# Conditioning columns as fp32 products over two load queues, and mixer products on half of the k tiles ahead of the last column

## The chip, the cores and the metric

The kernel runs on one core of a Trainium2 chip. The metric is device time in microseconds, from three runs, of which the median is taken; beside it stands one profiled execution, whose trace is what the rows below come from.

## What is computed

Two layers of a hybrid block on 256 latent tokens and 256 context tokens, 1024 features, fp32 throughout. Each layer turns a conditioning vector (one for latents, one for context) into shift, scale and gate, normalizes, mixes the tokens with four branches, and runs a convolutional feed-forward:

```python
mod = silu(c) @ p['w_ada'] + p['b_ada']            # 6 x 1024 columns: sh1, sc1, g1, sh2, sc2, g2
h = rmsnorm(x, p['norm1_g']) * (1 + sc1) + sh1     # c for the latents, c_ctx for the context
u = split_in(h @ p['w_in'])                        # SSD, GQA, differential attention, RG-LRU
y = merge_branches(h, (ssd, gqa, diff, rglru * gelu(gate)), p)
x = x + g1 * y
x = x + g2 * conv_ffn(modulate(rmsnorm(x, p['norm2_g']), sh2, sc2), p)
```

What matters here is the first stage: the mixer's input h of layer 0 needs x, its statistics, and the shift and scale of layer 0, and these need 1 MB x 8 of the weight w_ada.

## The kernel before

**Number format.** Products of the mixer take three passes: `whl` splits a weight into a high part (a cast to fp32r on ACT, L256, or on VectorE, L258) and a low part (a subtraction, L251, on VectorE or POOL); `split` does the same for activations; `mm3` (L265) multiplies low by high, high by low and high by high, and adds in PSUM. `turn` (L317) says which split takes POOL and which takes VectorE's cast. There are four buffers for split weights (`ws`) and two for raw ones (`wp`, tile `w`).

**First stage** (L1189 to L1243). Shift and scale of layer 0's first norm are 2048 columns, packed into four columns c of 512, each of four chunks of 512 KB, 16 chunks `ada0` to `ada15`. Column 0 is the shift of the features of k tiles 0 to 3, column 1 their scale, columns 2 and 3 the same for k tiles 4 to 7. A chunk holds two k tiles of the product, so it is two products of the conditioning (2 wide, the stationary operand) with 512 columns. Columns 0 and 1 are plain fp32 products (L1226), columns 2 and 3 are split and take three passes (L1224). All chunks load on SyncE's queue; eleven have a buffer `wa` each, the other five share the four `bo` buffers, so `ada15` waits for `ada11`. x comes in four loads on ACT's queue (`load_x`, L276), the parameter tables pp and rp there too (`load_params`, L358). `place` (L1202) copies a column's two rows from PSUM, turns them with four transposes and writes them into `mods`.

**Norm.** `norm_stats` (L497) squares x on ACT, sums on VectorE, and `rstd` (L477) gives 1/rms by a product with ones (L484), a power on POOL (L489) and a product that spreads it (L493). `norm_coeffs` (L455) makes scale and shift from `mods`, for half of the k tiles at a time. `norm` (L511) goes over the halves of the tokens (context first) and in each over the 8 k tiles: x times 1/rms (L517, into one of three `fo` buffers), scale and shift (L519 on ACT or L521 on VectorE), a cast (L256) and a subtraction (L251, POOL or VectorE): 16 tiles of 128x256 in all.

**Mixer.** `rg_in` (L987) is first: `rgx0` and `rgx1`, 1 MB each, two outputs each, and each output is `fm` (L525) over 8 k tiles, with `halves=True` for one half of the tokens after the other (256 columns a product, 192 products in all), then a convolution (`conv`, L542: ACT at L544, VectorE at L552). `rg_pair` (L1008) takes rgx0's two channels (tile `bcm`; rgx1's is `xs`): gate products (L1021, L1024), ACT, VectorE, one square root on ACT (L1033), scans (L1041 to L1044). `kvdt` and `xbc` follow.

**Order.** The program is written in order, but a planner orders each engine's instructions by its own estimate of when they are ready, the written order deciding among ready ones; on the chip each engine then runs its list in order. `tc.issue_after(i)` puts what it covers behind instruction i on that engine. A DMA is issued by an engine's own instruction list, and waits there if it has to.

Of the kernel before, what the change touches and what calls it, by code (L numbers as in the profile page):

```python
# [207 lines left out]
def _build(ctx, nc, tc, I, out, dbg):  # L208
# [56 lines left out]
    def mm3(ps, a, b, start, stop):  # L265

        PE.matmul(ps, a.l, b.h, start=start, stop=False)  # L267
        PE.matmul(ps, a.h, b.l, start=False, stop=False)  # L268
        PE.matmul(ps, a.h, b.h, start=False, stop=stop)  # L269

# [36 lines left out]
    def wraw(l, name, pl=None, tag=None, bufs=None, queue=None):  # L307
        off, kt, cols = CH[name]
        w = pl.tile([128, kt * cols], F32, name=tag, bufs=bufs) if pl else wp.tile([128, 2048], F32, name="w")
        t = I[f"w{l}"]  # L310
        (nc.scalar if pl and queue is None else nc.sync).dma_start(
            w[:, :kt * cols], bass.AP(tensor=t.tensor, offset=t.offset + off, ap=[[kt * cols, 128], [1, kt * cols]]))
        return w[:, :kt * cols].rearrange("p (k c) -> p k c", k=kt)
# [140 lines left out]

    def norm_coeffs(p, mod, base, gname, nm, halves=1):  # L455

        a = par.tile([128, 8, 2], F32, name=f"A{nm}")
        sh = par.tile([128, 8, 2], F32, name=f"sh{nm}")
        b = p["bada"]
        for i in range(halves):  # L460
            k = slice(i * 8 // halves, (i + 1) * 8 // halves)
# [5 lines left out]
        return a, sh  # L467

# [41 lines left out]

    def norm(x, rs, a, sh):  # L511
        h = Mat(*(hp.tile([128, KT, T], F32R, name=f"h{i}") for i in "hl"))
        for v, r in rs.items():
            ts = slice(v * 256, v * 256 + 256)
            for k in range(KT):
                t = tt("fo", 256)
# [7 lines left out]

    def fm(ps, w, h, n, start=True, stop=True, halves=False):  # L525

        if halves and n > 256:
            for v in reversed(range(n // 256)):
                ts = slice(v * 256, v * 256 + 256)
                fm(ps[:, ts], w, h[:, :, ts], 256)  # L530
            return
        kn = w.h.shape[1]
        for k in range(kn):
            mm3(ps, w[:, k], h[:, k, :n], start and k == 0, stop and k == kn - 1)

# [19 lines left out]
    class Mixer:  # L555
# [430 lines left out]

        def rg_in(self, i, tag, bufs):  # L987

            l, p, h = self.l, self.p, self.h
            w = wcols(l, f"rgx{i}")  # L990
            xr = self.long([128, 2, T], tag, bufs)
            bws = []
            for c in range(2):
                cp = 2 * i + c
                ps = big()
                fm(ps, w[c], h, T, halves=True)
                conv(xr[:, c], ps, p["rcw"], p["rcb"], T, 4, cp, 4)
# [196 lines left out]
    cth = ap_.tile([128, KT, 2], F32, name="cth")  # L1194
    csp = ap_.tile([128, 2, KT, 2], F32R, name="csp")
    cm = Mat(csp[:, 0], csp[:, 1])
# [3 lines left out]
    split(cm, ccol, V)  # L1200
    x = load_x()
    def place(c, ps):  # L1202
# [7 lines left out]
        V.tensor_copy(mods[0][:, i0:i0 + 4], tp.rearrange("p (i v) -> p i v", v=2))  # L1210

    before = None
    for c in range(4):

        ps = small()
        for k in range(0, KT, 2):
            z = c * 4 + k // 2
            w = wraw(0, f"ada{z}", ap_ if z < 11 else bop, "wa" if z < 11 else "bo", 11 if z < 11 else 4, nc.sync)
            w = w.rearrange("p a (k c) -> p (a k) c", k=2)
            if c >= 2:  # L1220
                w = whl(w)
            for i in range(2):
                if c >= 2:
                    mm3(ps[0:2], cm[:, k + i], w[:, i], k + i == 0, k + i == KT - 1)  # L1224
                else:
                    PE.matmul(ps[0:2], ccol[:, k + i], w[:, i], start=k + i == 0, stop=k + i == KT - 1)  # L1226
            if k == 2 and before:
                place(*before)
        before = c, ps
        if c == 2:  # L1230
            p = load_params(0)
            r = norm_stats(x, T)
    place(*before)
    closed(q0)
    for l in range(DEPTH):
        full = l < DEPTH - 1
        if l:
            p = load_params(l)
            with tc.high_priority():
                r = norm_stats(x, T)  # L1240
        with tc.issue_after(after[0, 4]) if l else nullcontext():
            a1, sh1 = norm_coeffs(p, mods[l], 0, "norm1", 1, 2)
        h = norm(x, r, a1, sh1)  # L1243
        early_params(l, p)
# [6 lines left out]
        b3 = mx.branch()  # L1251
        rin = [mx.rg_in(0, "bcm", 1), mx.rg_in(1, "xs", 2)]
        turn[1:] = 1, 2
# [68 lines left out]
        dbg(f"x{l}", x)  # L1322
        a2, sh2 = norm_coeffs(p, mods[l], 24, "norm2", 2)
        with tc.high_priority():
            h = norm(x, norm_stats(x, n), a2, sh2)
        fill = None
# [22 lines left out]
```

## Time and profile before

| what | us |
|---|---|
| median of three runs (1835.39 to 1839.09) | 1835.72 |
| the profiled execution | 1833.32 |
| its span, first to last instruction | 1831.2 |
| TensorE busy in the span | 1715.3 |
| VectorE, ACT, POOL busy | 1298.7, 904.4, 889.1 |

The profile gives each instruction's engine, line, tiles and times. A row of the timeline has its start and length in us, counted from the span's start; for several instructions merged into one row (xN) the length goes from the first start to the last end, or is their sum of covered time. Behind it, in brackets, stands the engine's idle time before the row and what ended it. "PE" is TensorE, "DVE" VectorE, "POOL" GpSimd, "SP" SyncE; a "q" behind an engine's name marks the issue of a DMA. A matmul's recorded length is longer than the step to the next one, as they are pipelined.

### The profile page before, as it was taken

To read this page: it belongs to the slowest core of one execution; us is meant where nothing else is said; L and a number is where in the kernel's file an instruction comes from. 1 tells how busy PE (TensorE), PEld (TensorE's weight loads), DVE (VectorE), ACT (ScalarE), POOL (GpSimd) and SP (SyncE) were. 2 spreads that over 40 slices of the span, in tenths; PEclk is the share of its full clock that TensorE was granted. 3 is DMA by queue.
4 is the path that set the end of the run, shared out by engine and by line. 5 is a ranking of instruction groups with operands and counts; after the bars stand their busy time and mean duration, and the time that the engine had idled before them with its cause. 6 is when DMAs were issued, how large, how long until landed. Compare 5 with 4: busy or idle time off the path is not lost.

```text
span 1831.2 us, 27922 instructions
## 1 busy us (share of the span) xinstructions
PE 1715.3 (94%) x10734; PEld 1499.3 (82%) x10734; DVE 1298.7 (71%) x2259; ACT 904.4 (49%) x1651; POOL 889.1 (49%) x536
## 2 busy tenths in 40 slices
PE   7968999999989998999999999966989999989999
PEld 1856788878788787987888888855888899989998
DVE  6798667666868676898856475698867668567664
ACT  3525544545444554465544343535445455556554
POOL 4364656252435657566543242465574244534443
PEclk8988999999989999999999999978989999989999
DMA  7211433131313355535645443222233133445553
GB/s 290 85 69 46 145 104 122 70 104 47 104 58 111 112 184 207 185 119 172 219 172 181 147 147 111 69 83 97 93 117 137 47 116 113 164 141 196 181 182 130
DMA packets 52036, 237.10 MB, mean 129 GB/s; under 512 B 9664, under 2 KB 12608, under 8 KB 34496
## 3 DMA queue, kind: packets, MB, share of 16 engines
q1 hardware_dynamic: 28080, 179.46, 28.1%
q10 hardware_dynamic: 23824, 55.86, 9.6%
q8 instruction: 85, 1.39, 0.3%
q14 instruction: 47, 0.39, 0.1%
HBM read 234.18 MB, written 1.11 MB: 128 GB/s over the span
## 4 chain that ended last, share of the span: by engine, by line
PE 44%; DVE 9%; DMA 2%; POOL 2%; ACT 2%; issue 2%; DVEq 0%; ACTq 0%; POOLq 0%; SPq 0%
PE big L267 13%; PE big L268 13%; PE big L269 13%; DVE whl L251 1%; DMA w<-in_w 1%; DVE fo L435 1%; POOL whl L251 1%; DVE fo L552 1%; DMA wa<-in_w 1%; PE small L781 1%; PE small L589 1%; ACT whl L256 1%; DVE whl L258 0%; DVE B L1044 0%; PE small L1021 0%
## 5 line engine op out<-in xcount | busy, mean ns | idle before, releaser
L251 POOL TENSOR_TENSOR whl<-w,whl 128x1024 fp32r<-128x1024 f32 (+3 forms) x194 | 453.8, 2342 | 525.8 <-ACT whl L256 428.5
L267 PE MATMUL big<-hh,whl 128*128 128x256 f32 (+1 forms) x1632 | 549.9, 341 | 25.6 <-POOL whl L251 22.7
L268 PE MATMUL big<-hl,whl 128*128 128x256 f32 (+1 forms) x1632 | 550.9, 339 | 0.8 <-POOL hl L251 0.8
L269 PE MATMUL big<-hh,whl 128*128 128x256 f32 (+1 forms) x1632 | 550.9, 339 | 0.0
L256 ACT CAST whl<-w 128x1024 fp32r<-128x1024 f32 (+2 forms) x314 | 308.5, 987 | 169.1 <-PE big L269 83.4
L267 PEld LDWEIGHTS big<-hh,whl 128*128 128x128 f32 x1632 | 313.2, 194 | 60.3 <-POOL whl L251 23.8
L268 PEld LDWEIGHTS big<-hl,whl 128*128 128x128 f32 x1632 | 314.3, 193 | 33.7 <-issue 2.8
L269 PEld LDWEIGHTS big<-hh,whl 128*128 128x128 f32 x1632 | 314.2, 193 | 33.1 <-issue 3.6
L251 DVE TENSOR_TENSOR whl<-w,whl 128x1024 fp32r<-128x1024 f32 (+2 forms) x150 | 206.3, 1377 | 68.6 <-ACT whl L256 68.3
L552 DVE SCALAR_TENSOR_TENSOR fo<-big,pp,fo 128x510 f32<-128x510 f32 (+2 forms) x224 | 141.4, 634 | 72.1 <-ACT fo L544 68.5
L431 POOL TENSOR_TENSOR wa<-wa,crow 128x1024 f32<-128x1024 f32 x48 | 125.9, 2626 | 75.5 <-DVE fo L435 44.2
L268 PE MATMUL big<-whl,hh 128*128 128x256 f32 (+1 forms) x512 | 149.6, 293 | 1.9 <-POOL whl L251 1.9
L267 PE MATMUL big<-whl,hl 128*128 128x256 f32 (+1 forms) x512 | 148.3, 291 | 2.3 <-DVE sq L1052 1.4
L269 PE MATMUL big<-whl,hh 128*128 128x256 f32 (+1 forms) x512 | 149.6, 293 | 0.0
L269 PE MATMUL big<-act,whl 128*128 128x256 f32 (+1 forms) x392 | 125.6, 321 | 0.0
L268 PE MATMUL big<-act,whl 128*128 128x256 f32 (+1 forms) x392 | 125.4, 320 | 0.0
L267 PE MATMUL big<-act,whl 128*128 128x256 f32 (+1 forms) x392 | 125.3, 320 | 0.0
L544 ACT ACTIVATE fo<-big,pp 128x512 f32<-128x512 f32 (+1 forms) x104 | 71.1, 684 | 90.4 <-PE big L269 82.3
L267 PE MATMUL big<-bo,whl 128*128 128x512 f32 (+1 forms) x256 | 89.3, 353 | 20.8 <-ACT bo L256 13.3
L268 PEld LDWEIGHTS big<-whl,hh 128*128 128x128 f32 x512 | 100.2, 196 | 3.8 <-POOL whl L251 2.1
L267 PEld LDWEIGHTS big<-whl,hl 128*128 128x128 f32 x512 | 100.0, 196 | 3.8 <-DVE sq L1052 1.7
L269 PEld LDWEIGHTS big<-whl,hh 128*128 128x128 f32 x512 | 100.3, 196 | 2.2 <-issue 2.1
(302 smaller groups left out, 3359.7 us busy)
## 6 DMA issues: line engine op xcount, KB each, us to landing
w<-in_w SPq DMA_DIRECT2D x136, 1024.0 KB, 4.9
wa<-in_w ACTq DMA_DIRECT2D x64, 512.0 KB, 3.6
w<-in_w SPq DMA_DIRECT2D x16, 768.0 KB, 4.2
w<-in_w SPq DMA_DIRECT2D x16, 640.0 KB, 3.8
bcm<-in_w ACTq DMA_DIRECT2D x14, 512.0 KB, 3.6
q<-csd ACTq DMA_DIRECT2D x24, 256.0 KB, 4.3
wa<-in_w SPq DMA_DIRECT2D x11, 512.0 KB, 8.5
xm<-in_xT ACTq DMA_DIRECT2D x8, 512.0 KB, 7.0
```

The lines of the kernel that those rows point to most:

```text
L251: eng.tensor_tensor(o, v, hi.bitcast(F32), op=OP.subtract)
L256: S.copy(m.h, v)
L267: PE.matmul(ps, a.l, b.h, start=start, stop=False)
L268: PE.matmul(ps, a.h, b.l, start=False, stop=False)
L269: PE.matmul(ps, a.h, b.h, start=False, stop=stop)
L431: G.tensor_tensor(w, w, cr, op=OP.mult)
L435: V.scalar_tensor_tensor(scr, w, 1.0, cr, op0=OP.mult, op1=OP.mult, accum_out=o)
L544: S.activation(o, ps, AF.Identity, scale=wt[:, nc_ + c:nc_ + c + 1], bias=b[:, c:c + 1])
L552: V.scalar_tensor_tensor(os_, is_, wt[:, j * nc_ + c:j * nc_ + c + 1], os_, op0=OP.mult, op1=OP.add)
L589: PE.transpose(ps[:, i * 128:(i + 1) * 128], s, ident)
L781: PE.matmul(ops[t][hs, pr * 128:(pr + 1) * 128], self.gv[:, k0 + kb, hs], ets[z][:, kb * 128:(kb + 1) * 128], start=kb == 0, stop=kb == kn ...
```

## The change

All four columns of conditioning are plain fp32 products, without split. Twelve chunks have a `wa` buffer and four a `bo` buffer, so none waits for another's; from chunk 6 on the odd chunks load on ACT's queue. `load_params` and `norm_stats` stand behind column 1 instead of column 2. Behind column 2 the coefficients and the norm of k tiles 0 to 3 are made, and `front(0)` multiplies rgx0 by those four k tiles, both halves of the tokens at once (512 columns a product, 24 products) into two PSUM tiles that stay open. The products of column 3 are placed behind the last of these on TensorE (`issue_after`). After column 3 has been placed, `front(1)` does the same for rgx1; coefficients and norm of k tiles 4 to 7 follow, and `rg_in` finishes the four open tiles with k tiles 4 to 7. Layer 1 keeps its instructions.

```diff
-        PE.matmul(ps, a.h, b.h, start=False, stop=stop)
+        return PE.matmul(ps, a.h, b.h, start=False, stop=stop)
...
-        (nc.scalar if pl and queue is None else nc.sync).dma_start(
+        (queue or (nc.scalar if pl else nc.sync)).dma_start(
...
-    def norm(x, rs, a, sh):
-        h = Mat(*(hp.tile([128, KT, T], F32R, name=f"h{i}") for i in "hl"))
+    def htile():
+        return Mat(*(hp.tile([128, KT, T], F32R, name=f"h{i}") for i in "hl"))
+
+    def norm(x, rs, co, h=None, ks=range(KT)):
+        a, sh = co
+        h = h or htile()
         for v, r in rs.items():
             ts = slice(v * 256, v * 256 + 256)
-            for k in range(KT):
+            for k in ks:
...
-        kn = w.h.shape[1]
-        for k in range(kn):
-            mm3(ps, w[:, k], h[:, k, :n], start and k == 0, stop and k == kn - 1)
+        for k in ks:
+            ins = mm3(ps, w[:, k], h[:, k, :n], k == 0, k == KT - 1)
+        return ins
...
-        def rg_in(self, i, tag, bufs):
+        def rg_in(self, i, tag, bufs, front=None):
...
-            w = wcols(l, f"rgx{i}")
+            w, pss = front or (wcols(l, f"rgx{i}"), None)
...
-                ps = big()
-                fm(ps, w[c], h, T, halves=True)
+                ps = pss[c] if front else big()
+                fm(ps, w[c], h, T, halves=not front, ks=range(4, KT) if front else range(KT))
...
+    def front(i):
+
+        w, pss = wcols(0, f"rgx{i}"), [big(), big()]
+        for c in range(2):
+            ins = fm(pss[c], w[c], h, T, ks=range(4))
+        return (w, pss), ins
+
...
-            w = wraw(0, f"ada{z}", ap_ if z < 11 else bop, "wa" if z < 11 else "bo", 11 if z < 11 else 4, nc.sync)
+            w = wraw(0, f"ada{z}", ap_ if z < 12 else bop, "wa" if z < 12 else "bo", 12 if z < 12 else 4,
+                     nc.scalar if z > 5 and z % 2 else nc.sync)
             w = w.rearrange("p a (k c) -> p (a k) c", k=2)
-            if c >= 2:
-                w = whl(w)
-            for i in range(2):
-                if c >= 2:
-                    mm3(ps[0:2], cm[:, k + i], w[:, i], k + i == 0, k + i == KT - 1)
-                else:
+            with tc.issue_after(ins.ins) if c == 3 else nullcontext():
+                for i in range(2):
                     PE.matmul(ps[0:2], ccol[:, k + i], w[:, i], start=k + i == 0, stop=k + i == KT - 1)
             if k == 2 and before:
                 place(*before)
         before = c, ps
-        if c == 2:
+        if c == 1:
             p = load_params(0)
             r = norm_stats(x, T)
+            co, h = coeffs(1), htile()
+        if c == 2:
+
+            norm_coeffs(p, mods[0], 0, "norm1", co, [(0, 4)])
+            norm(x, r, co, h, range(4))
+            turn[1] = NEVER
+            f0, ins = front(0)
     place(*before)
+    fronts = f0, front(1)[0]
...
-        h = norm(x, r, a1, sh1)
...
+        else:
+            norm_coeffs(p, mods[l], 0, "norm1", co, [(4, 8)])
+            norm(x, r, co, h, range(4, 8))
...
-        rin = [mx.rg_in(0, "bcm", 1), mx.rg_in(1, "xs", 2)]
+        rin = [mx.rg_in(0, "bcm", 1, fronts[0]), mx.rg_in(1, "xs", 2, fronts[1])]
```

## Rows read from the trace of the kernel before

**Rows 1.** The page's first part: busy us, share of span, instructions of each engine

```profile
PE 1715.3 (94%) x10734; PEld 1499.3 (82%) x10734; DVE 1298.7 (71%) x2259; ACT 904.4 (49%) x1651; POOL 889.1 (49%) x536
```

**Rows 2.** Table by stretches: length, busy of PE, PEld, DVE, ACT, POOL; PEclk; DMA; GB/s

```profile
20.00:30.00 10.00, 7.80 (x26) 2.33 (x24) 8.62 (x31) 3.52 (x4) 5.25 (x9) 0.83 1.03 417
...
40.00:50.00 10.00, 8.56 (x37) 4.28 (x38) 9.50 (x12) 1.05 (x1) 3.79 (x5) 0.67 0.12 29
```

**Rows 3.** Timeline of TensorE, 18 to 42 us: start, length, instruction, idle before

```profile
18.18 5.31 PE L1226 MATMUL small<-wa,ccol 128*2 128x512 f32 x12
...
25.50 0.61 PE L484 MATMUL small<-ones,tg 128*128 128x1 f32 x4
...
41.44 0.58 PE L268 MATMUL small<-whl,csp 128*2 128x512 f32 x1 [3.19 <-POOL whl L251]
```

**Rows 4.** Timeline of TensorE, 47 to 80 us

```profile
47.72 0.28 PE L267 MATMUL big<-hh,whl 128*128 128x256 f32 x1
...
51.39 0.41 PE L1208 MATMUL small<-cst,row 2*128 2x2 f32 x4
...
71.13 0.28 PE L269 MATMUL big<-hh,whl 128*128 128x256 f32 x1
...
79.66 0.59 PE L1021 MATMUL small<-bcm,q 128*128 128x512 f32 x1
```

**Rows 5.** Table by stretches, columns as in rows 2, around TensorE's pause

```profile
101.80:113.00 11.20, 0.09 (x2) 0.04 (x1) 11.20 (x15) 0.60 (x2) 8.02 (x7) 0.63 0.00 1
97.00:131.00 34.00, 20.07 (x94) 16.65 (x93) 32.80 (x50) 6.02 (x10) 24.54 (x15) 0.80 0.18 62
```

**Rows 6.** Waits of TensorE, 0 to 140 us: total, times, longest

```profile
PE big L267 <- POOL whl L251: 11.1, 1, 11.1
```

**Rows 7.** Groups by line, 20 to 48 us: count, busy us, mean ns, idle before

```profile
L268 PE MATMUL small<-whl,csp 128*2 128x512 f32 x16 | 7.7, 479 | 3.5 <-POOL whl L251 3.2 <-DVE whl L251 0.3
L251 DVE TENSOR_TENSOR whl<-bo,whl 128x1024 fp32r<-128x1024 f32 x4 | 5.2, 1301 | 0.0
...
L251 POOL TENSOR_TENSOR whl<-bo,whl 128x1024 fp32r<-128x1024 f32 x1 | 4.0, 3983 | 0.0
```

**Rows 8.** Timeline of SyncE's DMA issues: the last conditioning chunk

```profile
33.09 0.33 SPq L311 DMA_DIRECT2D bo<-in_w  x1
```

**Rows 9.** Waits of SyncE's DMA issues, 0 to 140 us

```profile
SPq L311 <- DMA rp<-in_rp: 1.0, 1, 1.0
```

**Rows 10.** Timeline of ACT, 9 to 11 us

```profile
9.99 0.34 ACTq L364 DMA_DIRECT2D rp<-in_rp  x1
10.37 0.42 ACT L503 ACTIVATE tg<-xm 128x256 f32<-128x256 f32 x1 [6.49 <-DMA xm<-in_xT]
```

**Rows 11.** Timeline of VectorE: last sum, tiles of the norm

```profile
20.65 0.41 DVE L507 TENSOR_TENSOR tg<-tg,sq 128x256 f32<-128x256 f32 x1
...
30.43 1.08 DVE L517 TENSOR_TENSOR fo<-xm,small 128x256 f32<-128x256 f32 x3 [1.32 <-PE small L493]
...
39.18 2.48 DVE L251 TENSOR_TENSOR hl<-fo,hh 128x256 fp32r<-128x256 f32 x1
...
52.44 0.74 DVE L521 TENSOR_SCALAR fo<-fo,A,sh 128x256 f32<-128x256 f32 x2
...
63.38 0.43 DVE L251 TENSOR_TENSOR hl<-fo,hh 128x256 fp32r<-128x256 f32 x1 [1.34 <-ACT hh L256]
```

**Rows 12.** Timeline of POOL, three stretches

```profile
33.61 3.83 POOL L251 TENSOR_TENSOR hl<-fo,hh 128x256 fp32r<-128x256 f32 x3
...
53.37 2.24 POOL L251 TENSOR_TENSOR hl<-fo,hh 128x256 fp32r<-128x256 f32 x3 [9.59 <-ACT hh L256]
...
110.12 10.69 POOL L251 TENSOR_TENSOR whl<-w,whl 128x1024 fp32r<-128x1024 f32 x4
```

**Rows 13.** Timeline of ACT: the first convolution, the square root

```profile
67.86 0.78 ACT L544 ACTIVATE bcm<-big,pp 128x512 f32<-128x512 f32 x1 [1.40 <-PE big L269]
...
92.05 1.92 ACT L1033 ACTIVATE B<-B 128x2048 f32<-128x2048 f32 x1
```

More of the change, by code (lines that the diff above doesn't have):

```diff
@@ L453, in finish, with coeffs, norm_coeffs @@
                 self()
-    def norm_coeffs(p, mod, base, gname, nm, halves=1):
-        a = par.tile([128, 8, 2], F32, name=f"A{nm}")
-        sh = par.tile([128, 8, 2], F32, name=f"sh{nm}")
+    def coeffs(nm):
+        return [par.tile([128, 8, 2], F32, name=f"{n}{nm}") for n in ("A", "sh")]
+    def norm_coeffs(p, mod, base, gname, co, runs=((0, 8),)):
+        a, sh = co
         b = p["bada"]
-        for i in range(halves):
-            k = slice(i * 8 // halves, (i + 1) * 8 // halves)
+        for k in runs:
+            k = slice(*k)
             s1, s2 = slice(base + k.start, base + k.stop), slice(base + 8 + k.start, base + 8 + k.stop)
@@ L466, in norm_coeffs @@
             V.scalar_tensor_tensor(a[:, k], a[:, k], 1.0, bc(p[gname][:, k, None], shape), op0=OP.add, op1=OP.mult)
-        return a, sh
+        return co
     def gate_coeffs(p, mod, base, f, nm):
@@ L509, in norm_stats @@
         return rs
-    def norm(x, rs, a, sh):
-        h = Mat(*(hp.tile([128, KT, T], F32R, name=f"h{i}") for i in "hl"))
+    def htile():
+        return Mat(*(hp.tile([128, KT, T], F32R, name=f"h{i}") for i in "hl"))
+    def norm(x, rs, co, h=None, ks=range(KT)):
+        a, sh = co
+        h = h or htile()
         for v, r in rs.items():
             ts = slice(v * 256, v * 256 + 256)
-            for k in range(KT):
+            for k in ks:
                 t = tt("fo", 256)
@@ L523, in norm, with fm @@
         return h
-    def fm(ps, w, h, n, start=True, stop=True, halves=False):
+    def fm(ps, w, h, n, halves=False, ks=range(KT)):
         if halves and n > 256:
@@ L529, in fm @@
                 ts = slice(v * 256, v * 256 + 256)
-                fm(ps[:, ts], w, h[:, :, ts], 256)
+                fm(ps[:, ts], w, h[:, :, ts], 256, ks=ks)
             return
-        kn = w.h.shape[1]
-        for k in range(kn):
-            mm3(ps, w[:, k], h[:, k, :n], start and k == 0, stop and k == kn - 1)
+        for k in ks:
+            ins = mm3(ps, w[:, k], h[:, k, :n], k == 0, k == KT - 1)
+        return ins
     def tm(ps, w, t, h):
@@ L1194, in _build @@
     cth = ap_.tile([128, KT, 2], F32, name="cth")
-    csp = ap_.tile([128, 2, KT, 2], F32R, name="csp")
-    cm = Mat(csp[:, 0], csp[:, 1])
     S.activation(cth, ccol, AF.Tanh, scale=0.5)
@@ L1199, in _build @@
     V.scalar_tensor_tensor(ccol, cth, 1.0, ccol, op0=OP.add, op1=OP.mult)
-    split(cm, ccol, V)
     x = load_x()
@@ L1240, in _build @@
                 r = norm_stats(x, T)
-        with tc.issue_after(after[0, 4]) if l else nullcontext():
-            a1, sh1 = norm_coeffs(p, mods[l], 0, "norm1", 1, 2)
-        h = norm(x, r, a1, sh1)
+            co = coeffs(1)
+            with tc.issue_after(after[0, 4]):
+                norm_coeffs(p, mods[l], 0, "norm1", co, [(0, 4), (4, 8)])
+            h = norm(x, r, co)
+            fronts = None, None
+        else:
+            norm_coeffs(p, mods[l], 0, "norm1", co, [(4, 8)])
+            norm(x, r, co, h, range(4, 8))
         early_params(l, p)
@@ L1322, in _build @@
         dbg(f"x{l}", x)
-        a2, sh2 = norm_coeffs(p, mods[l], 24, "norm2", 2)
+        co = norm_coeffs(p, mods[l], 24, "norm2", coeffs(2))
         with tc.high_priority():
-            h = norm(x, norm_stats(x, n), a2, sh2)
+            h = norm(x, norm_stats(x, n), co)
         fill = None
```

## The prediction

> **What bounds the kernel now.** The page's first part comes first: TensorE is busy for 94% of the span [rows 1], so over the whole kernel a change pays only where TensorE stands still or runs slowly. The edit touches only the first stage, so that stage is read by itself. The table by stretches shows it: from 20 to 30 us VectorE is busy for 8.62 of 10 us and the DMA engines are full (share 1.03, 417 GB/s), and from 40 to 50 us VectorE has 9.50 of 10 while TensorE's granted clock is 0.67, that is, partly at the lower of its levels of 1.2 and 2.4 GHz [rows 2]. TensorE's own timeline says why: the last conditioning products stand 3.19 us behind a POOL subtraction, and the mixer's first product starts at 47.72 [rows 3, 4]. Behind that, TensorE is packed until 71.13 + 0.28 = 71.4 us. The next thing to read is who profits when that moment moves. From 101.8 to 113.0 us TensorE does 0.09 us of work [rows 5], and the list of its waits names one wait of 11.1 us on the POOL half of a weight split [rows 6]. VectorE has 32.80 of the 34 us from 97 to 131 [rows 5]. So the stretch after the first products belongs to the chain convolution, ACT, VectorE scans, POOL, and a gain for TensorE alone is not the whole answer.
>
> **Part 1: conditioning columns 2 and 3 as fp32 products.** Removed are 8 weight splits (8 casts, 8 subtractions: 1301 ns on VectorE, 3983 ns for the POOL one in question [rows 7]) and 48 three-pass products, 16 of each kind, of 479 ns busy each [rows 7]. Added are 8 chunks of two fp32 products, each seen as two instructions: 32 instructions, at 5.31 / 12 = 0.44 us each as columns 0 and 1 run them now [rows 3]. That is 14.1 us of TensorE, 7.1 us per column, no less than the 11.1 us (48 x 0.23) that the old products cost at the full level. The fp32 form gives TensorE nothing; what it gives is that a product waits for its load alone. Of the 8 splits, about 5 x 1.3 + 4 x 0.7 = 9 us leave VectorE between 22 and 46 us. That is cover for the norm, not path, unless VectorE sets the norm's time, which it does there (below).
>
> **Part 2: loads.** The last chunk is issued at 33.09, since it waits for a buffer [rows 8]; a buffer each lets it follow the others. But the 16 DMA engines are full [rows 2], and chunks, x, tables and both rgx weights are 13.3 MB, at 0.41 MB per us some 33 us whichever queue carries them. I give the second queue nothing. It has a price: an issue waits for earlier landings, also those of the other queue (SP waits 1.0 us for rp, which ACT issued [rows 9]), and on ACT's queue the wait stands in ACT's own stream: the first square runs at 10.37, right behind the issue at 9.99 [rows 10]. Five issues more in that stream cost between 0 (placed behind the squares) and about 4 us (ahead of them; the squares now end around 20.4, and an issue can wait for landings until about 19). I take 0 to 2, in the start of the norm below. Here a rule speaks against the edit: the Trainium skill, "DMA: Bandwidth & Descriptors", section "Issuing engines are not separate DMA queues", says that issuing on several engines saves only the sequencer's issue time. By that rule alone the queue edit is worth nothing and costs nothing; the rows agree on the first and show a cost to ACT beside it.
>
> **Part 3: half the k tiles ahead.** Statistics: the last sum starts at 20.65 and ends at 21.06 [rows 11], but its product runs at 25.50 [rows 3], behind the split of a chunk, and the first normalized tile starts at 30.43 [rows 11]. In the new order that tile starts between 21.06 + 4.93 = 26.0 (the same steps, no queue ahead) and 30.4 (as now). I take 28, since the fp32 products of column 2, still waiting for loads at 22 to 27 us, share TensorE's queue. First half of the norm: 8 tiles (4 k tiles for each half of the tokens). The rows bound a tile from both sides: the 12 tiles that now follow the last coefficients take 52.44 to 63.81, 0.95 us each [rows 11]; the 4 ahead of them take 30.43 to 41.66, 2.8 us each, among weight splits [rows 11]. Two to four splits stay (rgx0 must be split before its products). I take 1.25 us, near the lower end as most splits go: 10 us, done at 38 (33.6 to 50).
>
> On the shared memory port: three POOL subtractions take 3.83 us beside VectorE's splits, 2.24 us without them [rows 12]. The Trainium skill, "SBUF — State Buffer", section "Who interferes with whom", says that a VectorE operation with two SBUF inputs and a POOL operation that reads SBUF exclude each other. By that rule POOL would need 0.75 us a tile once the splits are gone, and the first half would be done some 3 us sooner than I put it; the remaining splits of rgx keep me from it.
>
> Products: rgx0's 24 ahead-products follow the tiles and end about 4 us after the last tile: 42 (12 products, 0.25 to 0.4 us each, the second at a low clock). The last column waits for them by the new order: + 7.1 = 49.1. It now ends at 47.9, so **here nothing is gained**. Placing: from its end to the first scaled tile now takes 52.44 - 47.9 = 4.6 us, because 30 mixer products of 0.12 us stand ahead of the transposes at 51.39 [rows 4]; the bare steps are 1.7 us. I take 3: 52.1, level with 52.44. What has changed by then is what is left: 8 tiles instead of 12, at 0.95 us 7.6 us, done at 59.7 instead of 63.8; and for TensorE, besides rgx1's 24 ahead-products, which fill the norm's first 5 us, 48 products of N = 512. The 192 half-size products run in 47.72 to 71.41, 0.123 each, so 0.247 for one of full size: 11.8 us from the fifth tile on (52.1 + 4.8 = 56.9): **68.7 against 71.4, -2.7 us**. Nothing hides these 2.7: TensorE is packed before and after. rgx0's first output ends with the last tile, about 61, against 67.86, when its convolution starts now [rows 13]: -6 us for the chain that leads to the scan. One more product step stands out: the second channel's gate product starts at 79.66 [rows 4]; behind a group that ends at 68.7 it can start near 71.
>
> **The sum.** Two ends, then: -2.7 (TensorE) and -6 (the chain to ACT's square root at 92.05 [rows 13], then scans, then the POOL splits at 110.12 [rows 12] that end the wait of 11.1 us). The wait ends on the second chain but VectorE must also do the key and decay work, which comes from TensorE's products. I take the middle, -4.5. Layer 1 issues what it issued before, and nothing later is tied to a fixed time, so the shift should carry to the end. The profiled execution has 1833.3 us (span 1831.2): 1828.8. The three runs have a median 2.4 above it: **1831.2 us**.
>
> **Rivals.** (1) *More*: the statistics' product is not held up and tiles run at 0.95 us: first half done at 33.6, everything behind it 4.4 us sooner, TensorE -7, the chain -10; -10 in all, 1825.7. For it: 9 us less of VectorE work exactly there. Against: loads until 33 us. (2) *Hidden anyway*: TensorE starts sooner but VectorE, with 32.80 of 34 us from 97 to 131 [rows 5], and POOL's order hold the 113.0; 0 to -3, about 1834.5. (3) *Slower*: the last column behind the ahead-products. Everything from the first half's end H is serial: H + 4 + 7.1 + 3 + 4.8 + 11.8 = H + 30.7, against 71.4, so it decides at **H = 40.7**. With ACT's queue blocked to about 19 us, squares 4 us later, the statistics' product behind the last chunk of column 2 and tiles at 1.5 us, H is about 46: +5 us, 1841. For it: now the fourth tile alone ends at 41.66 [rows 11]. Against: the splits that delay it go.
>
> **How the numbers follow.** Forecast (-2 to -8) 0.42; more 0.14; hidden 0.24; slower 0.20. A measurement of this kernel can tell about 0.2%, 3.7 us, from no change. Of the forecast 0.36 lies beyond that and 0.06 within: faster 0.50, same 0.30, slower 0.20. The range takes in (1) with some more, as other work may be reordered by the planner: 1820, and (3) at its price: 1841.
>
> **What would show it.** Right: the last column's fp32 products start only behind 24 mixer products, near 42, and end near 49; 8 and not 12 tiles follow; the mixer's rgx products end near 68 to 69; the wait of 11.1 us on POOL ends 4 to 6 us sooner. Wrong: the first tile later than 30.4, or DMA issues on ACT between its squares (rival 3); the wait still ending near 113 (rival 2); more than 5 us saved at 71 (rival 1). A shift that is there at 130 us and gone at the end would break the last step of the sum.

## The result: 18 us slower

The changed kernel takes **1854.55 us** (median of four runs, 1853.66 to 1856.58) against 1836.38 for the kernel before in the same comparison: a ratio of 1.0098, 95% interval 1.0081 to 1.0116. A second comparison gave 1855.22 and 1.0113 [1.0097, 1.0128]. The forecast was 1831.2 and its range ended at 1841. The profiled execution has 1856.58, its span is 1854.7.

The page's first part and the table by stretches of the changed kernel (columns as in rows 1 and rows 2):

```profile
PE 1718.9 (93%) x10622; PEld 1490.2 (80%) x10622; DVE 1283.3 (69%) x2248; ACT 897.8 (48%) x1646; POOL 878.6 (47%) x534
```

```profile
20.00:30.00 10.00, 4.76 (x12) 1.90 (x13) 6.28 (x25) 5.71 (x14) 3.76 (x10) 0.58 1.02 417
...
60.00:70.00 10.00, 9.80 (x34) 3.65 (x32) 1.18 (x4) 0.00 (x0) 0.00 (x0) 1.00 0.00 0
70.00:80.00 10.00, 5.39 (x13) 4.28 (x14) 4.73 (x14) 5.20 (x12) 4.29 (x6) 0.66 0.25 60
118.40:129.60 11.20, 0.10 (x1) 0.10 (x1) 11.20 (x14) 0.55 (x2) 8.08 (x7) 0.60 0.00 1
```

TensorE is busy for only 3.6 us more than before, although the span is 23.5 us longer: the time was lost standing still, and 16.8 us of it are gone by the end of the first stage's rgx products. From 20 to 30 us it has 4.76 us of work where it had 7.80 [rows 2]. From 60 to 70 us the three other engines are nearly idle while TensorE works through conditioning, and from 70 to 80 us TensorE waits for them in turn, at a granted clock of 0.66. The pause that stood at 101.8 to 113.0 [rows 5] has kept its length and moved by 16.6 us.

**Where it begins: ACT.** Its timeline in the changed kernel (start, length; in brackets the idle time before and what ended it):

```profile
13.35 0.33 ACTq L311 DMA_DIRECT2D wa<-in_w  x1
13.73 0.42 ACT L505 ACTIVATE tg<-xm 128x256 f32<-128x256 f32 x1 [10.42 <-DMA xm<-in_xT]
...
15.90 2.15 ACTq L311 DMA_DIRECT2D wa<-in_w  x2
18.10 0.72 ACT L508 ACTIVATE sq<-xm 128x256 f32<-128x256 f32 x2 [3.34 <-DMA pp<-in_pp]
19.97 2.90 ACTq L311 DMA_DIRECT2D bo<-in_w  x2
22.91 0.72 ACT L508 ACTIVATE sq<-xm 128x256 f32<-128x256 f32 x2 [4.09 <-DMA wa<-in_w]
...
27.79 0.97 ACT L508 ACTIVATE sq<-xm 128x256 f32<-128x256 f32 x2
```

The issues of conditioning chunks stand between the squares. The squares then wait for the landing of pp and of a `wa` chunk, which no square reads: it is the issue ahead of them that waits. The first square is 3.4 us later than before [rows 10], the last ends at 28.76, where it ended at 20.4 before.

**How it spreads.** VectorE's copies around the four columns, and TensorE's timeline and waits:

```profile
24.23 0.67 DVE L1208 COPY row<-small 2x512 f32<-2x512 f32 x1
...
35.34 1.06 DVE L523 TENSOR_TENSOR fo<-xm,small 128x256 f32<-128x256 f32 x3
...
44.08 0.17 DVE L1213 COPY mod<-small 128x8 f32<-128x8 f32 x1 [4.54 <-PE small L1211]
...
44.68 0.73 DVE L527 TENSOR_SCALAR fo<-fo,A,sh 128x256 f32<-128x256 f32 x2
...
55.38 0.41 DVE L251 TENSOR_TENSOR hl<-fo,hh 128x256 fp32r<-128x256 f32 x1
...
69.83 0.17 DVE L1213 COPY mod<-small 128x8 f32<-128x8 f32 x1 [2.40 <-PE small L1211]
```

```profile
24.96 0.58 PE L1211 MATMUL small<-cst,row 2*128 2x2 f32 x4 [7.29 <-DVE row L1208]
...
37.77 0.71 PE L495 MATMUL small<-cst,rs 128*128 128x128 f32 x4 [2.17 <-POOL rs L491]
38.41 5.29 PE L1233 MATMUL small<-wa,ccol 128*2 128x512 f32 x8
43.64 0.41 PE L1211 MATMUL small<-cst,row 2*128 2x2 f32 x4
...
49.93 0.73 PE L267 MATMUL big<-hh,whl 128*128 128x512 f32 x2 [2.36 <-ACT hh L256]
...
58.95 0.39 PE L269 MATMUL big<-hh,whl 128*128 128x512 f32 x1
59.27 3.60 PE L1233 MATMUL small<-bo,ccol 128*2 128x512 f32 x8
...
74.61 2.07 PE L267 MATMUL big<-hh,whl 128*128 128x512 f32 x4 [4.81 <-ACT hh L256]
...
87.78 0.39 PE L269 MATMUL big<-hh,whl 128*128 128x512 f32 x1
```

The row copy of column 0 stands in VectorE's list behind a sum of squares, so the late squares hold up TensorE for 7.29 us at column 0's transposes. Column 1's transposes stand behind both spreads of 1/rms and eight of column 2's 16 product instructions (the row at 38.41), and run at 43.64; only then is there a scale for the first half of the norm (44.68). Its last tile ends at 55.8. Column 3 begins at 59.27, behind the mixer's products, its coefficients are in place at 70.0, and the rgx products end at 88.2 where they ended at 71.4 [rows 4]. From 69.8 to 74.6 TensorE has nothing.

### The profile page after: what moved, and what is told of

Same layout as the page of the kernel before. It is cut to its first block, busy times and chain, and to the rows that moved or that the text cites. A ratio compares the mean times of both kernels' runs of the same rounds, so it can differ in the third digit from the quotient of the medians.

```text
span 1854.7 us, 27669 instructions
## 1 busy us (share of the span) xinstructions
PE 1718.9 (93%) x10622; PEld 1490.2 (80%) x10622; DVE 1283.3 (69%) x2248; ACT 897.8 (48%) x1646; POOL 878.6 (47%) x534
## 4 chain that ended last, share of the span: by engine, by line
PE 38%; DVE 7%; DMA 2%; POOL 2%; ACT 2%; issue 1%; ACTq 0%; DVEq 0%; POOLq 0%; SPq 0%
PE big L267 11%; PE big L269 11%; PE big L268 11%; DMA w<-in_w 1%; DMA wa<-in_w 1%; POOL whl L251 1%; POOL wa L431 1%; PE small L787 1%; DVE whl L251 1%; PE small L595 1%; ACT whl L256 1%; DVE whl L258 0%; PE small L631 0%; DVE B L1050 0%; PE small L1027 0%
## 5 line engine op out<-in xcount | busy, mean ns | idle before, releaser
L267 PE MATMUL big<-hh,whl 128*128 128x256 f32 (+1 forms) x1600 | 545.2, 344 | 35.3 <-POOL whl L251 24.0
L267 PEld LDWEIGHTS big<-hh,whl 128*128 128x128 f32 x1600 | 306.9, 193 | 73.2 <-POOL whl L251 25.8
L268 PEld LDWEIGHTS big<-hl,whl 128*128 128x128 f32 x1600 | 307.6, 193 | 36.1 <-issue 3.7
L269 PEld LDWEIGHTS big<-hh,whl 128*128 128x128 f32 x1600 | 307.5, 192 | 34.3 <-issue 3.6
```

The lines of the kernel that those rows point to most:

```text
L269: return PE.matmul(ps, a.h, b.h, start=False, stop=stop)
```

## The experiments

Twelve runs followed the first result; three of them repeat a kernel for a second profile. The table holds the kernels, with the places that decide. "Column 1" and "column 3" are the times at which their coefficients stand in `mods`, H is the end of the norm's first half, "rgx" the end of the rgx products (all in us, one profiled execution each; the first, where there are two). The ratio is to runs of the kernel before on the same chip, whose median was 1834.6 to 1836.4. The last column is how much later than in the kernel before the first and the last of 96 row maxima of the attention run (315.7 and 1548.4 us there).

| kernel | median us | ratio, 95% interval | squares end | column 1 | H | column 3 | rgx | shift |
|---|---|---|---|---|---|---|---|---|
| before | 1836.4 | 1 | 20.4 | 27.1 | | 52.0 | 71.4 | 0, 0 |
| fp32 columns alone | 1834.5 | 0.9998 [0.9981, 1.0014] | 20.3 | 25.7 | | 46.3 | 66.1 | -5.6, +0.7 |
| changed, one queue, no order | 1837.9 | 1.0017 [1.0008, 1.0027] | 21.0 | 34.3 | 45.9 | 51.3 | 67.4 | +1.4, +4.2 |
| changed, one queue | 1848.3 | 1.0071 [1.0056, 1.0086] | 20.9 | 34.4 | 45.9 | 60.2 | 78.4 | +6.5, +15.0 |
| changed, no order | 1850.0 | 1.0078 [1.0058, 1.0097] | 29.0 | 44.5 | 56.0 | 61.4 | 77.5 | +11.5, +18.6 |
| changed | 1854.6 | 1.0098 [1.0081, 1.0116] | 28.8 | 44.2 | 55.8 | 70.0 | 88.2 | +16.4, +24.4 |
| before, two queues | 1842.9 | 1.0049 [1.0032, 1.0066] | 26.9 | 34.2 | | 59.6 | 78.9 | +7.3, +7.1 |
| changed, GpSimd's queue | 1855.3 | 1.0121 [1.0099, 1.0144] | 26.5 | 41.5 | 53.3 | 70.4 | 88.9 | +17.2, +25.6 |
| changed, one queue, early placing | 1852.9 | 1.0098 [1.0066, 1.0130] | 20.8 | 26.2 | 40.2 | 59.8 | 78.1 | +6.9, +18.6 |
| fp32 columns, early placing | 1835.6 | 1.0004 [0.9990, 1.0017] | 21.0 | 26.3 | | 54.2 | 74.0 | -1.1, -1.1 |
| before, column 3 twice | 1843.6 | 1.0044 [1.0029, 1.0058] | 21.2 | 27.9 | | 55.3 | 74.6 | +3.0, +14.3 |

Theory after the first result: rival 3, with two causes, ACT's stream blocked by the issues and column 3 held behind the products made ahead. The rival: one of them alone, or the fp32 products. The first four runs take them apart.

**One queue.** All chunks on SyncE, the rest as changed.

```diff
-                     nc.scalar if z > 5 and z % 2 else nc.sync)
+                     nc.sync)
```

> The changed kernel with all 16 conditioning chunks on SyncE's queue; nothing else differs. Theory Q (the loads on ACT's queue are the cause: their issues wait in ACT's stream and hold up the squares, whose last one ends at 28.8 us instead of 20.4): the last square ends near 20 to 21, the 192 or so rgx products end near 72 to 75 us instead of 88.2, and the time is 1836 to 1841, that is 14 to 18 us below the changed kernel. Theory O (column 3 behind the ahead-products is the cause, the queue is harmless): the rgx products still end beyond 82 and the time is 1848 or more. If both count, in between.

It took 1848.34 us, 6.2 below the changed kernel and 13 above before. TensorE's timeline of this kernel:

```profile
33.78 0.40 PE L1211 MATMUL small<-cst,row 2*128 2x2 f32 x4
...
40.07 0.73 PE L267 MATMUL big<-hh,whl 128*128 128x512 f32 x2 [2.36 <-ACT hh L256]
...
49.45 3.60 PE L1233 MATMUL small<-bo,ccol 128*2 128x512 f32 x8
...
64.79 2.08 PE L267 MATMUL big<-hh,whl 128*128 128x512 f32 x4 [4.81 <-ACT hh L256]
```

The same picture as above, each step 9.8 to 9.9 us earlier. So the second queue costs 9.9 us at every place of the first stage, and more than half of the loss is left without it by medians (at the first row maximum 6.5 of 16.4 us). By the rgx products (78.4) both theories have a part, as they lie between 75 and 82; the time is in theory O's range.

**No order.** Column 3 may run as soon as its chunks are there, two queues.

```diff
-            with tc.issue_after(ins.ins) if c == 3 else nullcontext():
+            with nullcontext():
```

> The changed kernel without the order that puts column 3 behind the ahead-products; the loads stay on two queues. Theory Q: the late squares stay (last one near 28.8 us), column 3 runs before the first mixer product, the rgx products end 5 to 7 us sooner than 88.2, time about 1848 to 1850. Theory O: time near 1838, the whole loss gone.

1850.01 us. H is as late as in the changed kernel (56.0), since ACT is blocked as there, and column 3's coefficients come at 61.4 instead of 70.0. The time is that of theory Q, but the rgx products end 10.7 us sooner, not 5 to 7.

**Neither.** Both edits.

> Both undone: all chunks on SyncE's queue and column 3 free to run before the ahead-products. Theory Q: as e1 or up to 4 us below it, 1832 to 1838. Theory O: as e2 to within 2 us, since the queue would be harmless.

1837.86 us, 2.7 above before. Both theories missed: it is 10.5 us below the run with one queue and 12.2 below the one with no order. What is left of the change here is the fp32 form, the earlier place of the statistics and the products made ahead. The rgx products end 4.0 us sooner than before, and the square root runs only 0.3 us sooner [rows 13]. VectorE's and ACT's timelines say why:

```profile
65.40 0.69 DVE L258 CAST whl<-w 128x1024 fp32r<-128x1024 f32 x1 [3.00 <-PE big L269]
66.01 1.53 DVE L558 SCALAR_TENSOR_TENSOR bcm<-big,pp,bcm 128x510 f32<-128x510 f32 x2
67.46 1.41 DVE L258 CAST whl<-w 128x544 fp32r<-128x544 f32 x1
68.78 1.39 DVE L558 SCALAR_TENSOR_TENSOR bcm<-big,pp,bcm 128x510 f32<-128x510 f32 x2
```

```profile
91.71 1.92 ACT L1039 ACTIVATE B<-B 128x2048 f32<-128x2048 f32 x1
```

The convolution of rgx0's outputs, which the gate products need, shares VectorE with casts of the next weights. TensorE is done early and stands from 67.4 to 70.28, where the first gate product starts; the trace names nothing that released it, but the row at 68.78 ends at 70.17, so the convolution is the likely one. So 4.0 us are 1.5 at the gate products and 0.3 at the square root. This is rival 2.

In the first stage the two causes add. At the rgx products the order costs 11.0 us with one queue and 10.7 with two, the queue 10.1 without the order and 9.8 with it. At the first row maximum the queue's cost is still whole (10.1 and 9.9), and of the order's about 5 are left (5.1 and 4.9), which fits the run with neither, whose earlier rgx products gained nothing. The medians do not add: the order costs 10.5 us with one queue (1848.3 - 1837.9) and 4.5 with two, the queue 12.2 without the order and 6.2 with it. That difference arises behind the first row maximum, where each kernel's shift goes on to change (last column of the table, and below); it does not show that one cause hides the other.

**The queue on the kernel before.** One part alone: the same odd chunks on ACT's queue.

```diff
-        (nc.scalar if pl and queue is None else nc.sync).dma_start(
+        (queue or (nc.scalar if pl else nc.sync)).dma_start(
...
-            w = wraw(0, f"ada{z}", ..., nc.sync)
+            w = wraw(0, f"ada{z}", ..., nc.scalar if z > 5 and z % 2 else nc.sync)
```

> The kernel before with one part of the change alone: from chunk 6 on the odd chunks load on ACT's queue (its three-pass products, its 11 buffers and its order of work stay). Theory Q: the last square ends 4 to 8 us later than 20.4 and the time is 3 to 9 us above before. Theory O: the same as before within 3 us. A rival to both, that ACT's delay is hidden here because the 1/rms has to wait for TensorE's queue until 25.5 anyway: squares later, time unchanged.

1842.88 us, ratio 1.0049. ACT's waits and timeline:

```profile
ACT tg L503 <- DMA bo<-in_w: 14.7, 1, 14.7
```

```profile
13.25 2.88 ACTq L311 DMA_DIRECT2D wa<-in_w  x2
18.40 0.34 ACTq L364 DMA_DIRECT2D rp<-in_rp  x1
18.79 0.42 ACT L503 ACTIVATE tg<-xm 128x256 f32<-128x256 f32 x1 [14.69 <-DMA bo<-in_w]
```

Here the first square runs at 18.79, 8.4 us later than before [rows 10], behind issues alone. TensorE's transposes wait 9.2 us for row copies on VectorE in all, where it was 1.9. So theory Q held, and the delay was not hidden.

**The odd chunks on GpSimd's queue.** A second queue, but no issue among ACT's squares.

```diff
-                     nc.scalar if z > 5 and z % 2 else nc.sync)
+                     nc.gpsimd if z > 5 and z % 2 else nc.sync)
```

> The changed kernel with the odd chunks from the seventh on issued by GpSimd instead of ACT: there is still a second queue, but ACT's stream holds none of these issues. Theory A (the harm is that an issue that waits for an earlier landing stands among ACT's squares): the squares end near 21 as with one queue, not 28.8, the statistics come at 24 and 28, and the time is that of one queue, 1846 to 1850. Theory B (two queues take the DMA engines from x and the chunks that are needed first): the squares end late again, 25 or more, and the time stays at 1853 to 1856. GpSimd has its own work from about 30 us, so up to 2 us may be lost there under A.

Theory A failed and theory B held: 1855.28 us, as slow as the changed kernel, with the last square at 26.5. ACT's waits:

```profile
ACT tg L505 <- DMA xm<-in_xT: 9.5, 1, 9.5
ACT sq L508 <- DMA xm<-in_xT: 5.0, 2, 3.1
ACT sq L508 <- DVE tg L509: 1.9, 2, 1.5
```

Now the squares wait for x itself. GpSimd issues its five chunks from 1.3 us on, beside x, and the four loads of x take 6.7 to 16.1 us to land instead of 6.8 to 11.8 with one queue. TensorE's conditioning products wait for chunks as well, 11.5 us in four waits instead of 6.3 in one. So there are two mechanisms, one for each place of the queue: on ACT the issue blocks the squares (in the changed kernel all of x had landed by 16 us), on GpSimd the chunks take the DMA engines from x. What a second queue can't do is add bandwidth, as the prediction had it from rows 2; the Trainium skill, "DMA: Bandwidth & Descriptors", section "Issuing engines are not separate DMA queues", says that such transfers run on the same 16 engines and interleave, and this run agrees: from 5 to 30 us the engines moved 405 GB/s here and 400 with one queue. One thing stays open: H comes 2.5 us sooner than in the changed kernel, and column 3 no sooner (70.4).

**Early placing.** One queue, and each column placed right behind its own products.

```diff
-            if k == 2 and before:
-                place(*before)
-        before = c, ps
+        place(c, ps)
```

> The changed kernel with all chunks on SyncE's queue, and each column placed directly behind its own products instead of behind the first chunks of the next column; column 3 still waits for the products made ahead. With one queue alone, column 1's coefficients came at 34.4 and the first half of the norm ended at 45.9. Theory A (the late placing of column 1 is what sets the first half): its coefficients come near 28, the first half ends near 40, column 3 ends some 6 us sooner than in the run with one queue (56.9), the rgx products end near 72 (78.4 there), and the time is about 1841 to 1843 against 1848.3. Theory B (the tiles themselves, on VectorE and POOL, set it): the first half still ends near 45, and the time stays within 2 us of 1848.3.

Half of theory A held. Column 1 is in place at 26.2 and H falls from 45.9 to 40.2, so the placing was what held the first half. But column 3's coefficients come as late as before (59.8 against 60.2), because the transposes now stand behind other work:

```profile
46.79 7.03 PE L1233 MATMUL small<-bo,ccol 128*2 128x512 f32 x16
53.75 0.50 PE L267 MATMUL big<-hh,whl 128*128 128x512 f32 x1
...
59.21 0.41 PE L1211 MATMUL small<-cst,row 2*128 2x2 f32 x4
...
64.43 2.07 PE L267 MATMUL big<-hh,whl 128*128 128x512 f32 x4 [4.38 <-ACT hh L256]
```

23 of the products made ahead for rgx1 run between column 3's last product and its transposes, 5.5 us. The time is 1852.88 us. That is 4.5 above the run with one queue, but the intervals of the two ratios overlap. The first stage ends within 0.3 us of that run; in the profiled execution the shift grows from 8.5 to 12.1 us between 550 and 700 us while that of the run with one queue grows from 8.5 to 9.3, and this kernel has another order of instructions on VectorE and ACT between 500 and 700 us too.

**The fp32 columns alone**, with 12 and 4 buffers, one queue, nothing ahead; and the same with early placing.

```diff
-            if c >= 2:
-                w = whl(w)
...
-                if c >= 2:
-                    mm3(ps[0:2], cm[:, k + i], w[:, i], k + i == 0, k + i == KT - 1)
-                else:
-                    PE.matmul(ps[0:2], ccol[:, k + i], w[:, i], start=k + i == 0, stop=k + i == KT - 1)
+                PE.matmul(ps[0:2], ccol[:, k + i], w[:, i], start=k + i == 0, stop=k + i == KT - 1)
```

> The kernel before with one part of the change alone: all four conditioning columns as fp32 products, 12 and 4 buffers for their tiles, all chunks issued by SyncE; no product is made ahead. If the loss comes from the second queue and from the order of column 3, as the four runs so far say (+8 and +10 us), this kernel has neither and is not slower than before: columns 2 and 3 lose 8 weight splits, the last coefficient comes some 2 to 4 us sooner than 52.4, the rgx products end near 68 to 71, and the time is 1831 to 1836. If the fp32 products themselves cost something (TensorE held for 7.1 us a column at the low clock), the time is 1838 or more, as in the kernel with both undone (1837.9).

> The run with fp32 columns alone, and beside it each column placed directly behind its own products. Nothing is made ahead, one queue. If the placing is on the path of the norm, its first scaled tile comes earlier than in the run with fp32 columns alone by 1 to 4 us and the time is lower by 1 to 4 us, about 1829 to 1834; if the chain of VectorE and POOL behind it hides that, the two agree within 1.5 us.

Alone: 1834.52 us, no measurable difference. But its first stage is the fastest of all kernels. TensorE, and the table by stretches:

```profile
34.87 3.59 PE L1218 MATMUL small<-bo,ccol 128*2 128x512 f32 x8
38.39 0.41 PE L1205 MATMUL small<-cst,row 2*128 2x2 f32 x4
38.73 3.59 PE L1218 MATMUL small<-bo,ccol 128*2 128x512 f32 x8
42.25 0.38 PE L267 MATMUL big<-hh,whl 128*128 128x256 f32 x1
```

```profile
40.00:50.00 10.00, 10.00 (x70) 7.94 (x69) 7.26 (x16) 2.45 (x6) 2.18 (x3) 1.00 0.55 176
```

(The buffers of the chunks differ as well. But the last chunk, issued at 33.09 before [rows 8], had landed 4.3 us later, and here its products run only from about 40.5, which speaks against the buffers as the cause.) Column 3 ends at 42.3 instead of 47.9, without the 3.19 us pause for the POOL split [rows 3], and TensorE is busy from 40 to 50 us at a granted clock of 1.00 instead of 8.56 us at 0.67 [rows 2]. The rgx products end at 66.1, 5.3 us sooner than before. With early placing the transposes wait for row copies on VectorE and the statistics for the transposes; the granted clock is 0.66 from 35 to 50 us, column 3's 16 instructions take 9.47 us instead of 7.2, and the gain is gone: the expected 1 to 4 us came out as a loss in the first stage and as nothing in the time (1835.64).

So a gain of 5.3 us in the first stage does not show in the median. The next four runs ask whether that is chance.

**Second profiles** of the kernel before, of the fp32 columns alone and of the changed kernel, nothing edited.

> The kernel before once more, unchanged, for a second profiled execution of it and a direct measure of how far two executions of one kernel differ. The profiled execution of fp32 columns alone is 5.4 us ahead of that of before from 75 to 375 us, and 0.4 us behind it at the end, while the loss comes in steps of about 1.4 us where the granted clock of a stretch differs (0.98 against 1.00 at 900 to 1000 us). Theory A (executions differ by themselves): the two executions of before agree within 0.5 us up to 375 us, and part by 2 us or more by the end, in such steps. Theory B (an earlier start is given back by a tie to something later): the two agree within 1 us at every place up to the end. The ratio is 1.000 within 0.002 either way.

> The fp32 columns alone once more, for a second profiled execution and a narrower interval. Theory A (executions differ by themselves): 5 to 6 us ahead of before at 75 to 375 us again, but the later loss is at other places and of another size than 5.8 us, and over 5 rounds the time is 2 to 5 us below before. Theory B (given back by a tie): the same 5.8 us go again at the same places, and the time is that of before within 1.5 us.

> The changed kernel once more, for a second profiled execution. The first one was 16.4 us behind before from 150 to 375 us and 23.5 at the end. Theory A (executions differ by themselves): 16 to 17 us at 150 to 375 us again, and at the end anything from 14 to 24, with the median of the times near 1853. Theory B (later stages lose more because the stage before them is late): 23 again at the end, by the same steps.

**A plain delay**: the kernel before, with column 3's products made a second time into a PSUM tile that nobody reads.

```diff
                 if c >= 2:
+                    if c == 3:
+                        if k + i == 0:
+                            pd = small()
+                        mm3(pd[0:2], cm[:, k + i], w[:, i], k + i == 0, k + i == KT - 1)
                     mm3(ps[0:2], cm[:, k + i], w[:, i], k + i == 0, k + i == KT - 1)
```

> The kernel before, with the 24 products of conditioning column 3 made a second time into a buffer that nobody reads. Nothing is moved and no load changes; TensorE has about 5.5 us more to do (24 x 0.23 at the full clock, up to 11 at the lower level) just ahead of the mixer's first products. This gives the price of work put ahead of column 3's coefficients, and what the later stages make of a plain delay. Theory A (a delay of the first stage carries to the end as it is): column 3 ends 5 to 8 us later, everything from 75 to 375 us is that much later, and the end too, within 1.3 us, the difference of two executions of before; time 1841 to 1844. Theory B (any displacement changes the stretches of lower granted clock behind it): the same delay up to 375 us, but at the end 2 us more or less than that. Theory C (the coefficients are not on the path): column 3 is later, and the rgx products end within 1 us of 71.4.

The row maxima of the attention: count, shortest, median, longest duration in ns, first and last start in us. In this order the kernel before, its second profile, the fp32 columns alone, the plain delay and the changed kernel:

```profile
L738 DVE TENSOR_REDUCE mx<-small x96: 406/676/693, 315.7 to 1548.4; 128x1 f32<-128x512 f32 x64, 128x1 f32<-128x256 f32 x32
```

```profile
L738 DVE TENSOR_REDUCE mx<-small x96: 405/676/693, 314.5 to 1547.9; 128x1 f32<-128x512 f32 x64, 128x1 f32<-128x256 f32 x32
```

```profile
L738 DVE TENSOR_REDUCE mx<-small x96: 406/676/693, 310.1 to 1549.1; 128x1 f32<-128x512 f32 x64, 128x1 f32<-128x256 f32 x32
```

```profile
L738 DVE TENSOR_REDUCE mx<-small x96: 404/676/693, 318.7 to 1562.7; 128x1 f32<-128x512 f32 x64, 128x1 f32<-128x256 f32 x32
```

```profile
L744 DVE TENSOR_REDUCE mx<-small x96: 405/675/694, 332.1 to 1572.8; 128x1 f32<-128x512 f32 x64, 128x1 f32<-128x256 f32 x32
```

The two executions of the kernel before differ by 1.2 us at the first and 0.5 at the last. Between them lie 1.2 to 1.4 us from 75 to 850 us, and then a step of 2.0, so neither theory on them fits.

The fp32 columns alone are 5.6 us ahead and then 0.7 behind; their second profile 4.6 ahead and 1.8 behind. The gain is given back, and twice (by medians too: 1834.52 and 1836.04, ratios 0.9998 and 0.9996). The steps are in part at the same places, as theory B had it: in both executions the lead falls by about 1 us at 400 us and by nearly 3 from 850 to 950, though of the latter the second execution of the kernel before loses 2.0 too. Is it another order of instructions? From 125 to 252 us this kernel's engines do run in another order than before, but the lead is about the same ahead of it and behind it (5.4 and 5.7). From 260 to 1290 us VectorE, ACT and POOL have the order of the kernel before, and there the lead falls from 5.7 us (at 300) to 0.7 (at 1200), in the second execution from 4.7 to 0.9 behind.

The changed kernel's second execution is 17.0 us behind at the first row maximum and 21.3 at the last, where the first had 16.4 and 24.4; theory A held (16 to 17, then 14 to 24), but for the median, 1855.22 instead of about 1853. Its VectorE, ACT and POOL too have the order of the kernel before from 100 to 1147 us, and its shift grows there to 21.0 and 18.3.

The plain delay shows that a shift need not stay what it is even when nothing else changes. It costs 3.0 us in the first stage (less than the 5.5 expected; the granted clock there is 1.00 and not 0.67 from 40 to 50 us), and 14.3 by the last row maximum of its profiled execution, which was the slowest of its five; its median, 1843.55, is 8.9 above before. Yet TensorE, VectorE, ACT and POOL run the same instructions in the same order in both traces from about 100 us to the end. The waits of TensorE from 720 to 760 us and from 908 to 962 tell two of the places, for the plain delay:

```profile
PE big L268 <- DVE mm L251: 4.5, 2, 3.3
...
PE big L267 <- POOL whl L251: 3.7, 1, 3.7
```

In the kernel before the first is one wait of 1.0 us and the second is not there. The second wait is 1.8 us in that kernel's second profile, 3.0 and 1.1 in the two of the changed kernel, and 3.5 and 2.2 in the two of the fp32 columns alone. So the later stages hold products that wait for a split which is only just in time, and how long they wait differs with the shift, but also between two executions of one kernel. What sets it when the order is the same stays open; the granted clock differs at some places too (400 to 500 us: 0.98 in both executions before, 0.96 in both of the fp32 columns alone), but which comes first was not shown. Of the changed kernel's 18 to 19 us, then, 16.4 to 17.0 are explained by the first stage, and the rest is not.

## Why the prediction was wrong, step by step

**What bounds the kernel** was read at the right place: the loss arose in the first stage, and the pause that ends with the POOL split came 16.6 us later at its old length.

**Part 1, the fp32 columns, was undersized.** A column took 7.2 us as forecast (7.1). But "the fp32 form gives TensorE nothing" failed: without the splits column 3 ends 5.6 us sooner and TensorE runs at the full clock there (fp32 columns alone). The cost of the old form had been counted in products only, not in the pause before them, nor in the lower clock at which they ran behind it. (VectorE also had six of the subtractions between 22 and 46 us, not about five.) None of this gain is left at the end, against the last step of the sum.

**Part 2, the queue, is the first step that failed.** The price was put at 0 to 4 us and taken as 0 to 2; it was 9.9 us in the first stage (one queue against two), and 6.2 us in the median with the order, 12.2 without it. The mechanism was named, issues that wait in ACT's stream, but its size came from the squares alone and from a last wait at 19 us. ACT's last issue ended at 22.9, the squares 7.8 us late against one queue. And VectorE's list was not followed: behind the late sums stands the row copy of column 0, and TensorE stood 7.29 us for it.

**Part 3, the start of the norm's first half, is the second.** The prediction started the tiles at 28 from the statistics alone and did not ask when column 1's coefficients come, which stood at 27.1 before. In the new order they come at 34.4 with one queue and 44.2 with two, because their transposes stand in TensorE's list behind the statistics and column 2's products; early placing moved H by 5.7 us, which shows it. H was 55.8 instead of 38: by the coefficients of column 1, some 10 us are the queue's and some 7 the placing's, and the tiles themselves (44.7 to 55.8, 1.4 us each instead of 1.25) add 1.

**Behind H the steps held.** Column 3 started at H + 3.4 (forecast 4, to the end of the ahead-products), took 7.45 with a set of transposes in it (7.1), was placed 3.3 later (3), the next product came 4.6 after that (4.8). The last 48 products took 13.6 instead of 11.8: the prediction had priced them at the full level, and behind the pause the granted clock was 0.66. In all H + 32.4 instead of H + 30.7. The sum's other end, the chain to ACT's square root, was forecast 6 us sooner; the square root ran 16.5 us later (108.58 against 92.05).

**The rivals.** It was rival 3, at a chance of 0.20 and with the right point of decision: H = 40.7 decides, and the run with one queue came out at the H of 46 that the rival assumed and at 78.4, near its 76.7. That bears out the serial chain behind H; that H itself agrees is luck, for the rival reached 46 by a blocked ACT and slow tiles, and this run has a free ACT and the late coefficients of column 1, which no rival names. With ACT blocked too they add, and H is 56. So the upper end of the range was short by 13.6 us. Rival 2 was seen in the run with neither cause: 4.0 us gained at the rgx products, 0.3 at the square root. That the split work leaves VectorE, the argument for the forecast, was true (6.28 us from 20 to 30 instead of 8.62) and gained nothing in this kernel, where VectorE waits for other engines instead (4.54 us for column 1's transposes).

**The signs** named as wrong both appeared: issues between ACT's squares, and a first tile, at 35.3, later than 30.4. The shift at 130 us was not gone at the end but larger, 16.5 and 23.5 between the two profiled executions; by medians it is 18 to 19. So the sum's last step, that a shift carries to the end as it is, failed too.

## What to carry to other kernels

When a step is brought forward, list every input of its first instruction, and for each the engine lists that it now stands in: the norm's statistics were moved up, and the column that it also needed was thereby moved back. An order that puts the last input of a serial chain behind work made ahead delays that input by the work (column 3's coefficients by 8.6 to 8.9 us here, of which about 5 reached the later stages), so work made ahead should fill gaps, not stand ahead of what the rest waits for. A DMA issue on a computing engine is a wait in that engine's stream; one queue on SyncE, which computes nothing, cost none of it here. Putting the issues behind what is urgent on ACT was not tried.

## What the runs showed of the hardware that was not expected

- An issue on ACT's queue held the engine for up to 4.09 us in the changed kernel and moved the first square to 18.79 us in the kernel before, while x had landed.
- More transfers at once delay each: with five chunks issued early from GpSimd the slowest load of x took 16.1 us instead of 11.8.
- The 16 fp32 product instructions of one column took 7.03 us in one kernel, at a granted clock of 1.00, and 9.47 in another, in a stretch with 0.66 (one queue and fp32 columns, both with early placing).
- The two profiled executions of the kernel before agreed within 1.4 us from 75 to 850 us, and one of them had a wait of 1.8 us at a weight split behind 900 us that the other had not. A shift of 3 us by useless products in the first stage, with the order behind it unchanged, grew to 14 us in one execution and 9 in the median. A saving of 5 us was given back. A measured difference of some us is therefore not proof of what a change does in its own stage; the trace of that stage is.
